# State-space input tables computed in their final position instead of being transposed

## The chip, the cores and the metric

The kernel runs on one core of a Trainium2 chip. The metric is device time in microseconds (us) of one execution: the median of three runs of the kernel before is 2120.89 us (2119.84 to 2126.75).

## What is computed

The reference is one layer of a hybrid decoder trunk on 256 tokens of width 2048: a SwiGLU feed-forward block, a mixer (a state-space model "S5" beside sparse attention), and a second feed-forward block, each between RMS norms. The change touches only the small tables of the S5 part. They depend on parameters alone, not on the tokens:

```python
dt = exp(log_dt); lam_re = min(a_re, -1e-4); mag = exp(lam_re * dt)
ab_re, ab_im = mag * cos(a_im * dt), mag * sin(a_im * dt)          # one complex factor per state
co_re, co_im = ((ab - 1) / lam)                                     # complex division, written out
bb_re = co_re[..., None] * b_re - co_im[..., None] * b_im
bb_im = co_re[..., None] * b_im + co_im[..., None] * b_re
bu = einsum('btgc,gpc->tbgp', ug, bb)                               # input of the recurrence
x = scan(x * ab + bu);  y = Re(einsum(x, c)) + d_skip * ug
```

There are 64 groups of 16 channels with 64 complex states each. The kernel takes four tokens at a time, so that its input table holds bb times the factor ab to the powers 3, 2, 1 and 0.

## The kernel before

All matmuls run as three products of split numbers: a weight tile ("raw", 128x1024 floats, 512 KB) is loaded by SyncE's queue (SP), ScalarE (ACT) rounds it into "hi" (line 103), VectorE (DVE) computes the rest "lo" (line 105), and TensorE (PE) multiplies hi and lo (lines 278 to 280). Below, **item n** is the n-th such weight tile of the stream; one item is 12 matmuls in the first stage. Five raw buffers and four pairs of hi and lo hold what is ahead, so the hi of item n can only be written when PE has finished item n-4.

The stages are: the first feed-forward block (a gate block and an up block of 8 items each for every 512 columns, then a down projection), the mixer, the second feed-forward block. In the first feed-forward block, while PE streams weights, a list of small steps called `background` is worked off by `pump`: one or two steps per item. The steps are the S5 parameters (`s5_params`, lines 742 to 819: some 90 VectorE instructions on 128x32, and two Sin on ScalarE), the attention bias table (`bias_table`: a load of 2 KB on ScalarE's queue, 12 small GpSimd instructions, a write and a 3 MB broadcast, lines 922 to 931), and then, for each of 8 column tiles `ct`:

- `loads` (lines 846 to 855): two loads of 128 KB, power 0 of the input table `bd`, the start of the output table `gb`;
- `b_power` three times (lines 860 to 862): the next power of `bd`, three VectorE instructions on 128x256 each;
- `into` (lines 871 to 876): 8 transposes of `bd` on PE (line 322), two copies from PSUM by ScalarE (line 875), a 512 KB write to `s5in` in DRAM;
- `c_power` four times (lines 867 to 869) and `out_of` (lines 884 to 896): 8 matmuls, two VectorE copies, 16 GpSimd copies into `hz` (line 892), three writes to `s5out`.

The mixer reads both tables back later. The gate block's Silu is line 690 and the product with the up block line 691; both read the PSUM banks `acc`, of which there are four, so that the third block (gate of the second 512 columns, items 17 to 24) can only start in a bank after line 690 has read it.

What sets the order of instructions on each engine is a scheduler at build time, which works with a model of the durations; each engine then runs its list strictly in that order. A DMA that ScalarE's queue issues stands in ScalarE's list too and holds up what follows while it waits.

```python
hl = self._pair()                                # 4 pairs of hi and lo
self.rounded.append(nc.scalar.activation(h, r, AF.Copy).ins)
self.rest = nc.vector.tensor_tensor(l, r, h.bitcast(F32), op=ALU.subtract).ins
pump(1 + (kk % 8 == 0))                          # steps of background per item
S.activation(sg, g[t], AF.Silu, scale=rr(t))     # frees the gate block's bank
```

Of the kernel before, what the change touches and what calls it, by code (L numbers as in the profile page):

```python
# [173 lines left out]
def body(tc, a):  # L174
# [651 lines left out]
    in_dram = dp.tile([8, 128, 1024], F32, name="s5in")  # L826
    out_dram = dp.tile([8, 128, 1536], F32, name="s5out")

    def s5_tables(sp_):
# [11 lines left out]
        state = {}  # L841

        def loads(ct):
# [4 lines left out]
            state["bd"] = sp_.tile([128, 2, 4, 4, 32], F32, name="bd")  # L848
            state["gb"] = sp_.tile([128, 2, 4, 5, 32], F32, name="gb")
            b0, bd, gb = state["b"], state["bd"], state["gb"]  # L850
            V.tensor_tensor(t1, b0, bc(cor, ct, False), op=ALU.mult)
            V.tensor_tensor(t2, b0[:, ::-1], bc(coi2, ct, True), op=ALU.mult)
            V.tensor_tensor(bd[:, :, :, 3, :], t1, t2, op=ALU.add)
# [16 lines left out]

        def into(ct):
            bt = sp_.tile([128, 2, 512], F32, name="bt")
            for r in range(2):
                p = transpose4(state["bd"][:, r].rearrange("p q j c -> p (q j c)"))
                S.activation(bt[:, r], p, AF.Copy)
            nc.scalar.dma_start(in_dram[ct], bt.rearrange("p r s -> p (r s)"))

        def out_of(ct):
# [3 lines left out]
            for q in range(4):  # L882
                for r in range(2):
                    T.matmul(hp[32 * q:32 * q + 32], bd[:, r, q, 3, :],
                             gb[:, r, q, 0:4, :], start=r == 0, stop=r == 1, tile_position=(0, 32 * q))
# [14 lines left out]
        def at_start(f):  # L900
            with tc.issue_after(start):
                f()

        background.append(lambda: at_start(s5_params))
        background.append(bias_table)
        for ct in range(8):
            background.append(lambda ct=ct: loads(ct) if ct else at_start(lambda: loads(0)))
            for j in (2, 1, 0):
                background.append(lambda ct=ct, j=j: b_power(ct, j))
            background.append(lambda ct=ct: into(ct))  # L910
# [521 lines left out]
def layout(i):  # L1432
# [7 lines left out]
    for n in ("ffn1", "ffn2"):  # L1440
# [23 lines left out]
    d["ssm_b"] = np.ascontiguousarray(np.stack(  # L1464
        [_block_diag(f["ssm_b_re"]), _block_diag(f["ssm_b_im"])], axis=2)).reshape(8, 128, 256)
    d["ssm_c"] = np.ascontiguousarray(np.stack(
        [_block_diag(f["ssm_c_re"].transpose(0, 2, 1)), _block_diag(f["ssm_c_im"].transpose(0, 2, 1))],
# [21 lines left out]
```

## Time and profile before

| | |
|---|---|
| runs | 2120.89, 2119.84, 2126.75 us |
| profiled execution, its own time | 2120.92 us |
| its span, first to last instruction | 2119.2 us |
| PE busy | 2096.6 us, 99% of the span |
| VectorE busy | 1572.3 us, 74% |
| ScalarE busy | 1115.5 us, 53% |
| granted TensorE clock, mean | 0.999 |
| moved by DMA | 437.63 MB, 207 GB/s |

Busy shares are averages over stages. Matmuls are pipelined, so the duration of one (0.39 us for 128x512) is longer than the distance from one start to the next, which is the price of one more matmul in a row. All other times below are in us from the span's start.

### The profile page before, as it was taken

Reading aid. Unit: us, or ns where it says so; the run is one execution under the profiler, and the core shown is the slowest. Engines: PE = TensorE matmul, PEld = TensorE weight load, DVE = VectorE, ACT = ScalarE, POOL = GpSimd, SP = SyncE. Lnnn points to the kernel's source line nnn. Section 1 sums busy time; section 2 is a strip of 40 time slices with the busy share of each in tenths; the row PEclk is TensorE's granted clock in tenths of the full one; section 3 lists DMA queues with packets and bytes.
Section 4 is the critical chain, followed back from the end, with each engine's and each line's share of the span. In section 5 each row is a group of like instructions: output and inputs, shape, how many; then the busy total and the mean of one; then the engine's idle time right before and its main releaser. Section 6 shows DMA issues by size and latency. Waiting matters only on the chain.

```text
span 2119.2 us, 27930 instructions
## 1 busy us (share of the span) xinstructions
PE 2096.6 (99%) x10048; PEld 1726.9 (81%) x10048; DVE 1572.3 (74%) x2268; ACT 1115.5 (53%) x1537; POOL 273.3 (13%) x494
## 2 busy tenths in 40 slices
PE   8999999999999999999999999999999999999998
PEld 7887788888888878998787778888878888888886
DVE  7898788886867864454456656577898889778676
ACT  6444455555555565554445554465555555555453
POOL 1222300000000002993104320000000000000000
PEclk9999999999999999999999999999999999999999
DMA  8877656565665766567754346676556665656665
GB/s 285 268 239 234 202 196 211 197 213 180 205 206 198 272 205 225 163 223 248 276 165 139 122 144 214 203 268 184 188 191 197 208 197 190 219 170 210 217 207 179
DMA packets 137146, 437.63 MB, mean 207 GB/s; under 512 B 14880, under 2 KB 27312, under 8 KB 136880
## 3 DMA queue, kind: packets, MB, share of 16 engines
q1 hardware_dynamic: 117504, 403.10, 58.0%
q10 hardware_dynamic: 19504, 32.75, 4.5%
q8 instruction: 79, 1.29, 0.2%
q14 instruction: 59, 0.48, 0.1%
HBM read 417.42 MB, written 21.52 MB: 207 GB/s over the span
## 4 chain that ended last, share of the span: by engine, by line
PE 81%; POOL 8%; DVE 5%; issue 2%; DMA 2%; ACT 1%; ACTq 0%; DVEq 0%; SPq 0%; POOLq 0%
PE bank L524 15%; PE bank L525 15%; PE bank L523 15%; PE acc L278 10%; PE acc L279 10%; PE acc L280 10%; DVE lo L105 2%; POOL st L1005 2%; POOL sc L1002 2%; PE xp L322 2%; POOL sc L1003 1%; POOL st L1004 1%; DMA raw<-in_ffn_gu 1%; POOL hz L892 1%; DMA s5out<-gb 1%
## 5 line engine op out<-in xcount | busy, mean ns | idle before, releaser
L105 DVE TENSOR_TENSOR lo<-raw,hi 128x1024 fp32r<-128x1024 f32 (+3 forms) x676 | 796.7, 1186 | 353.7 <-ACT hi L103 352.2
L103 ACT ACTIVATE hi<-raw 128x1024 fp32r<-128x1024 f32 (+3 forms) x676 | 686.1, 1023 | 682.1 <-PE acc L280 306.8
L278 PE MATMUL acc<-hi,ah 128*128 128x512 f32 (+2 forms) x1072 | 414.9, 388 | 2.0 <-ACT hi L103 1.9
L279 PE MATMUL acc<-lo,ah 128*128 128x512 f32 (+2 forms) x1072 | 413.9, 386 | 0.0
L280 PE MATMUL acc<-hi,al 128*128 128x512 f32 (+2 forms) x1072 | 412.6, 385 | 0.0
L524 PE MATMUL bank<-lo,ah 128*128 128x512 f32 x758 | 296.7, 391 | 2.3 <-DVE lo L105 2.3
L525 PE MATMUL bank<-hi,al 128*128 128x512 f32 x746 | 290.7, 390 | 0.0
L523 PE MATMUL bank<-hi,ah 128*128 128x512 f32 x758 | 282.0, 391 | 0.0
L278 PEld LDWEIGHTS acc<-hi,ah 128*128 128x128 f32 x1072 | 201.4, 188 | 42.8 <-ACT hi L103 2.7
L279 PEld LDWEIGHTS acc<-lo,ah 128*128 128x128 f32 x1072 | 201.7, 188 | 38.9 <-issue 2.1
L280 PEld LDWEIGHTS acc<-hi,al 128*128 128x128 f32 x1072 | 201.6, 188 | 38.3 <-DVE al L351 0.3
L524 PE MATMUL bank<-lo,hT 128*128 128x512 f32 x520 | 202.5, 389 | 0.0
L525 PE MATMUL bank<-hi,hT 128*128 128x512 f32 x520 | 202.3, 389 | 0.0
L523 PE MATMUL bank<-hi,hT 128*128 128x512 f32 x520 | 190.7, 390 | 0.1
L524 PEld LDWEIGHTS bank<-lo,ah 128*128 128x128 f32 x758 | 142.4, 188 | 32.5 <-DVE lo L105 3.5
L523 PEld LDWEIGHTS bank<-hi,ah 128*128 128x128 f32 x758 | 142.3, 188 | 29.3
L525 PEld LDWEIGHTS bank<-hi,al 128*128 128x128 f32 x746 | 140.1, 188 | 28.7
L103 ACT ACTIVATE hi<-sums 128x1024 fp32r<-128x1024 f32 x84 | 88.5, 1054 | 63.0 <-DVE sums L140 29.7
L523 PEld LDWEIGHTS bank<-hi,hT 128*128 128x128 f32 x520 | 97.5, 188 | 21.1 <-ACT hi L103 0.9
L524 PEld LDWEIGHTS bank<-lo,hT 128*128 128x128 f32 x520 | 97.6, 188 | 20.2
L525 PEld LDWEIGHTS bank<-hi,hT 128*128 128x128 f32 x520 | 97.6, 188 | 20.1
L105 DVE TENSOR_TENSOR lo<-sums,hi 128x1024 fp32r<-128x1024 f32 x84 | 101.0, 1217 | 3.9 <-ACT hi L103 3.1
(322 smaller groups left out, 2674.3 us busy)
## 6 DMA issues: line engine op xcount, KB each, us to landing
raw<-in_ffn_gu SPq DMA_DIRECT2D x352, 512.0 KB, 4.3
raw<-in_ffn_d SPq DMA_DIRECT2D x176, 512.0 KB, 4.3
raw<-in_w_ya SPq DMA_DIRECT2D x64, 512.0 KB, 3.4
raw<-in_w_in SPq DMA_DIRECT2D x40, 512.0 KB, 4.1
raw<-in_w_gate_b SPq DMA_DIRECT2D x32, 512.0 KB, 3.7
raw<-in_w_out SPq DMA_DIRECT2D x32, 512.0 KB, 3.8
raw<-in_w_o SPq DMA_DIRECT2D x16, 512.0 KB, 3.9
tab<-s5out ACTq DMA_DIRECT2D x8, 768.0 KB, 6.5
```

The source lines that it names most:

```text
L103: self.rounded.append(nc.scalar.activation(h, r, AF.Copy).ins)
L105: self.rest = nc.vector.tensor_tensor(l, r, h.bitcast(F32), op=ALU.subtract).ins
L278: T.matmul(o, lh, wh[:, k, :], start=kk + k == 0, stop=False)
L279: T.matmul(o, lh, wl[:, k, :], start=False, stop=False)
L280: last_product[0] = T.matmul(o, ll, wh[:, k, :], start=False, stop=kk + k == nk - 1).ins
L322: last_transpose[0] = T.transpose(p[:, k, :], src[:, k * cols:(k + 1) * cols], ident).ins
L523: T.matmul(out, lh, wh[:, j, :], start=key not in self.started, stop=False)
L524: T.matmul(out, lh, wl[:, j, :], start=False, stop=False)
L525: last_product[0] = T.matmul(out, ll, wh[:, j, :], start=False, stop=last).ins
L892: G.tensor_copy(hq[32 * j:32 * j + 32, q, j:, :], hs[32 * q:32 * q + 32, 0:4 - j, :])
L1002: G.tensor_tensor(w[:, 0], x, a4r2, op=ALU.mult)
L1005: G.tensor_tensor(y, y, w[:, 1], op=ALU.add)
```

## The change

The input table is computed in the position that the matmul wants, channels on partitions and states on the free axis. The inputs are laid out turned on the host (`ssm_bt`, repeated four times over the partitions, one copy for each power), and the complex factors, co times ab to the powers 0 to 3, are put into rows: `coefs` computes them for all groups at once (20 VectorE instructions on 128x32), transposes them with two matmuls, copies them three times by ScalarE (one of them negated) and writes 128x384 floats to `k_dram` ("s5k"). For each column tile, four loads on ScalarE's queue then broadcast a 6 KB row of it to 32 partitions each (`kt`), and one load of 512 KB brings the turned input (`bt0`). `into` becomes two halves of three VectorE instructions on 128x512. The 24 `b_power` steps, the 64 transposes and their 16 copies are gone. `coefs` stands before `bias_table` in the list.

```diff
+        def coefs():
+            w = work().rearrange("p (r j c) -> p r j c", r=4, j=4)
+            k, t = w[:, 0:2], w[:, 2:4]
+            tt = V.tensor_tensor
+            V.tensor_copy(k[:, 0, 3], cor)
+            V.tensor_copy(k[:, 1, 3], coi2[:, 1])
+            for j in (2, 1, 0):
+                xr, xi = k[:, 0, j + 1], k[:, 1, j + 1]
+                tt(t[:, 0, 0], xr, ar, op=ALU.mult)
...
+            p = transpose4(k.rearrange("p r j c -> p (r j c)"), n=2)
+            rows = work().rearrange("p (v s) -> p v s", v=4)
+            S.activation(rows[:, 0], p[:, 0], AF.Copy)
+            S.activation(rows[:, 1], p[:, 1], AF.Copy, scale=-1.0)
+            S.activation(rows[:, 2], p[:, 1], AF.Copy)
+            nc.scalar.dma_start(k_dram, rows[:, 0:3].rearrange("p v s -> p (v s)"))
...
+            nc.scalar.dma_start(state["bt"].rearrange("p r q s -> p (r q s)"), a["ssm_bt"][ct])
+            for j in range(4):
+                src = k_dram[32 * j + 4 * ct:32 * j + 4 * ct + 4].rearrange("q n -> (q n)")
+                nc.scalar.dma_start(state["k"][32 * j:32 * j + 32].rearrange("p q v s -> p (q v s)"),
+                                    src.unsqueeze(0).to_broadcast([32, 1536]))
...
-        def b_power(ct, j):
-            bd = state["bd"]
-            src = bd[:, :, :, j + 1, :]
-            V.tensor_tensor(t1, src, bc(ar, ct, False), op=ALU.mult)
-            V.tensor_tensor(t2, src[:, ::-1], bc(ai2, ct, True), op=ALU.mult)
-            V.tensor_tensor(bd[:, :, :, j, :], t1, t2, op=ALU.add)
...
-        def into(ct):
-            bt = sp_.tile([128, 2, 512], F32, name="bt")
-            for r in range(2):
-                p = transpose4(state["bd"][:, r].rearrange("p q j c -> p (q j c)"))
-                S.activation(bt[:, r], p, AF.Copy)
-            nc.scalar.dma_start(in_dram[ct], bt.rearrange("p r s -> p (r s)"))
+        def into(ct, half):
...
+            V.tensor_tensor(y, x[:, :, qs], k[:, qs, 0].unsqueeze(1).to_broadcast([128, 2, 2, 128]), op=ALU.mult)
+            V.tensor_tensor(t, x[:, ::-1, qs], k[:, qs, 1:3].rearrange("p q v s -> p v q s"), op=ALU.mult)
+            V.tensor_tensor(y, y, t, op=ALU.add)
+            if half:
+                nc.scalar.dma_start(in_dram[ct], state["in"].rearrange("p r q s -> p (r q s)"))
...
         background.append(lambda: at_start(s5_params))
+        background.append(coefs)
         background.append(bias_table)
```

The scheduler's lists move with it. Below are three places, first of ScalarE. This is ScalarE's list before from the load of the bias table on (`rel_bias`, line 922); the two lines 690 are the Silu of the gate block for the two token tiles:

```order
L922 DMA wk<-in_rel_bias 16x32
L350 ACTIVATE ah_135<-xp,gains 128x128
L103 ACTIVATE hi<-raw 128x1024
L690 ACT_TABLE_LOAD
L690 ACTIVATE wk<-acc,r_415 128x512
L930 DMA rb_one<-wk 16x384
L103 ACTIVATE hi<-raw 128x1024
L931 DMA rb<-rb_one 128x6144
L784 ACTIVATE wk<-wk 128x32
L103 ACTIVATE hi<-raw 128x1024
```

And this is ScalarE's list of the change up to the hi of item 21. The rows ahead of it are the hi of items 18 to 20, a load for the second column tile and the three copies of `coefs` (lines 862 to 864). Line numbers are the changed kernel's: 865 is the write of `coefs`, 879 a load of `kt`, 876 the load of `bt0` for the second column tile, 906 the write of `s5in`; 952 to 961 are the bias table:

```order
L952 DMA wk<-in_rel_bias 16x32
L865 DMA s5k<-wk 128x384
L690 ACT_TABLE_LOAD
L690 ACTIVATE wk<-acc,r_416 128x512
L690 ACTIVATE wk<-acc,r_429 128x512
L879 DMA kt<-s5k 32x1536 x4
L960 DMA rb_one<-wk 16x384
L961 DMA rb<-rb_one 128x6144
L876 DMA bt_850<-in_ssm_bt 128x1024
L879 DMA kt<-s5k 32x1536
L906 DMA s5in<-bt 128x1024
L103 ACTIVATE hi<-raw 128x1024
```

The first Silu stood right behind the hi of item 15; it now stands behind the hi of item 20, behind the copies and the write of `coefs`, with a second table load (one more stands at the Sin, line 784). Between the hi of item 20 and that of item 21 lie twelve DMA issues. Three more loads of `kt` follow behind the hi of item 21.

On PE this is the list of the change at the end of item 16 (the last of the first up block); in the list before, the same place reads the same without the row of line 322:

```order
L279 MATMUL acc<-lo,ah_136 128x512
L280 MATMUL acc<-hi,al_137 128x512
L322 MATMUL xp<-ident,wk 128x128 x2
L278 MATMUL acc<-hi,ah_134 128x512
L279 MATMUL acc<-lo,ah_134 128x512
```

The two transposes of `coefs` stand between item 16 and item 17, the first item of the next gate block.

On VectorE this is the list of the change from the lo of item 20 on (854 to 859 are `coefs`, 812 to 819 the end of `s5_params`):

```order
L105 TENSOR_TENSOR lo<-raw,hi 128x1024
L815 TENSOR_TENSOR a4r_112<-wk 128x32
L816 TENSOR_SCALAR a4i_113<-wk 128x32
L854 TENSOR_TENSOR wk<-wk,ar 128x32
L855 TENSOR_TENSOR wk<-wk,ai_109 128x32
L857 TENSOR_TENSOR wk<-wk,ai_109 128x32
L858 TENSOR_TENSOR wk<-wk,ar 128x32
L818 COPY a4r_112<-a4r_112 128x32
L819 TENSOR_SCALAR a4i_113<-a4i_113 128x32
L856 TENSOR_TENSOR wk<-wk 128x32
L859 TENSOR_TENSOR wk<-wk 128x32
L854 TENSOR_TENSOR wk<-wk,ar 128x32
```

Five more small instructions end `coefs`, so that it is done only 16 small instructions behind the lo of item 20. Behind it stand the two of line 691, the six of `into` of the first column tile (902 to 904), five of `c_power` on 128x256, and then the lo of item 21. Ahead of it, 17 instructions (15 on 128x32, two on 128x256) lie between the lo of item 19 and that of item 20, where before there were four.

## Rows read from the trace of the kernel before

**Rows 1.** The page's first part: busy time, share of the span and instructions of each engine.

```profile
PE 2096.6 (99%) x10048; PEld 1726.9 (81%) x10048; DVE 1572.3 (74%) x2268; ACT 1115.5 (53%) x1537; POOL 273.3 (13%) x494
```

**Rows 2.** The waits of PE alone over the whole span: line, what it waited for, us in total, times, longest.

```profile
PE xp L322 <- DMA wk<-in_x: 5.4, 2, 5.1
PE bank L524 <- DVE lo L105: 2.9, 4, 1.1
PE xp L322 <- DVE bd L862: 2.2, 1, 2.2
PE acc L278 <- ACT hi L103: 1.9, 2, 1.4
```

**Rows 3.** Busy time by stretch: length, then each engine's busy us (and instructions), granted clock, DMA share, GB/s. The stretch from 57 to 240 is that of the column tiles; 13 to 16 is the kernel's opening.

```profile
57.00:240.00 183.00, 180.75 (x940) 146.71 (x939) 158.62 (x312) 79.19 (x91) 47.59 (x113) 1.00 0.74 240
13.00:16.00 3.00, 3.00 (x19) 2.53 (x18) 2.23 (x6) 2.35 (x6) 0.00 (x0) 1.00 1.04 408
```

**Rows 4.** PE in order of time around the first group of eight transposes: start, duration, instruction.

```profile
70.62 0.39 PE L280 MATMUL acc<-hi,al 128*128 128x512 f32 x1
70.85 1.03 PE L322 MATMUL xp<-ident,bd 128*128 128x128 f32 x8
71.64 0.48 PE L278 MATMUL acc<-hi,ah 128*128 128x512 f32 x1
71.96 0.39 PE L279 MATMUL acc<-lo,ah 128*128 128x512 f32 x1
```

**Rows 5.** Groups of instructions from 0 to 420: times, busy us and mean ns of one, idle time before them.

```profile
L322 PE MATMUL xp<-ident,bd 128*128 128x128 f32 x64 | 8.3, 273 | 2.3 <-DVE bd L862 2.2
L860 DVE TENSOR_TENSOR t<-bd,ar 128x256 f32<-128x256 f32 x24 | 10.6, 440 | 0.1
L567 DVE TENSOR_TENSOR wk<-bank,wk 128x512 f32<-128x512 f32 x4 | 2.8, 692 | 0.7 <-PE bank L525 0.3
L350 ACT ACTIVATE ah<-xp,gains 128x128 fp32r<-128x128 f32 x32 | 11.1, 382 | 8.6 <-DVE al L351 4.4 <-PE xp L322 3.9
```

**Rows 6.** The time around the one idle stretch of PE in the column tiles, all engines: start, duration, instruction, and in brackets the idle time before it with its releaser.

```profile
212.56 11.51 POOL L892 COPY hz<-hs 32x32 f32<-32x32 f32 x16 [17.53 <-DVE hs L887]
224.56 2.95 ACT L103 ACTIVATE hi<-raw 128x1024 fp32r<-128x1024 f32 x3 [8.32 <-POOL hz L892]
225.65 1.23 DVE L105 TENSOR_TENSOR lo<-raw,hi 128x1024 fp32r<-128x1024 f32 x1 [4.82 <-ACT hi L103]
228.15 1.06 PE L322 MATMUL xp<-ident,bd 128*128 128x128 f32 x8 [2.22 <-DVE bd L862]
```

**Rows 7.** PE in order of time where item 16 ends and item 17 begins.

```profile
56.34 0.39 PE L280 MATMUL acc<-hi,al 128*128 128x512 f32 x1
56.57 0.39 PE L278 MATMUL acc<-hi,ah 128*128 128x512 f32 x1
```

**Rows 8.** ScalarE in order of time (ACTq is its queue issuing a DMA): the hi of item 15 and the first Silu with its table load, the hi of item 20, and a pair of DMA issues later on.

```profile
39.37 1.06 ACT L103 ACTIVATE hi<-raw 128x1024 fp32r<-128x1024 f32 x1 [0.28 <-PE acc L280]
40.44 1.28 ACT L690 ACT_TABLE_LOAD   x1
41.74 0.69 ACT L690 ACTIVATE wk<-acc,r 128x512 f32<-128x512 f32 x1
56.82 1.06 ACT L103 ACTIVATE hi<-raw 128x1024 fp32r<-128x1024 f32 x1 [1.08 <-PE acc L280]
119.28 0.94 ACTq L895 DMA_DIRECT2D s5out<-gb  x2
```

**Rows 9.** VectorE in order of time: an instruction on 128x256 and what follows, small ones in a row, and the lo of item 19 with what follows it.

```profile
53.94 0.42 DVE L851 TENSOR_TENSOR t<-ld,cor 128x256 f32<-128x256 f32 x1
54.28 0.18 DVE L804 TENSOR_TENSOR wk<-wk 128x32 f32<-128x32 f32 x1
54.50 0.19 DVE L805 TENSOR_TENSOR coi<-wk 128x32 f32<-128x32 f32 x1
54.61 0.19 DVE L814 TENSOR_TENSOR wk<-ar,ai 128x32 f32<-128x32 f32 x1
55.44 1.22 DVE L105 TENSOR_TENSOR lo<-raw,hi 128x1024 fp32r<-128x1024 f32 x1
56.58 0.74 DVE L691 SCALAR_TENSOR_TENSOR wk<-acc,r,wk 128x512 f32<-128x512 f32 x1
```

**Rows 10.** PE in order of time in its first stretch of matmuls, after it had been idle.

```profile
10.01 0.63 PE L280 MATMUL acc<-hi,al 128*128 128x512 f32 x1
10.43 0.63 PE L278 MATMUL acc<-hi,ah 128*128 128x512 f32 x1
10.86 0.61 PE L279 MATMUL acc<-lo,ah 128*128 128x512 f32 x1
```

**Rows 11.** DMA issues over the whole span: times, KB each, median us from issue to landing; and the landing times of the writes of `s5out`, least, median and greatest.

```profile
s5out<-gb ACTq DMA_DIRECT2D x16, 256.0 KB, 4.4
rb_one<-wk ACTq DMA_DIRECT2D x1, 24.0 KB, 2.1
wk<-in_rel_bias ACTq DMA_DIRECT2D x1, 2.0 KB, 3.3
DMA to landing us min/median/max: 2.0/4.2/7.1
```

**Rows 12.** GpSimd on the bias table, in order of time.

```profile
40.44 3.63 POOL L928 TENSOR_SCALAR wk<-wk 16x5 f32<-16x5 f32 x11
```

More of the change, by code (lines that the diff above doesn't have):

```diff
@@ L827, in body @@
     out_dram = dp.tile([8, 128, 1536], F32, name="s5out")
+    k_dram = dp.tile([128, 384], F32, name="s5k")
     def s5_tables(sp_):
@@ L847, in loads @@
                 state[nm] = w
[L848 removed]
+            state["bd"] = sp_.tile([128, 2, 4, 32], F32, name="bd")
             state["gb"] = sp_.tile([128, 2, 4, 5, 32], F32, name="gb")
[L850 removed]
+            state["bt"] = sp_.tile([128, 2, 4, 128], F32, name="bt0")
+            state["k"] = sp_.tile([128, 4, 3, 128], F32, name="kt")
+            nc.scalar.dma_start(state["bt"].rearrange("p r q s -> p (r q s)"), a["ssm_bt"][ct])
[3 more added lines that the diff above has]
+                                    src.unsqueeze(0).to_broadcast([32, 1536]))
+            b0, gb = state["b"], state["gb"]
             V.tensor_tensor(t1, b0, bc(cor, ct, False), op=ALU.mult)
             V.tensor_tensor(t2, b0[:, ::-1], bc(coi2, ct, True), op=ALU.mult)
[L853 removed]
+            V.tensor_tensor(state["bd"], t1, t2, op=ALU.add)
             V.tensor_copy(gb[:, 0, :, 0, :], state["c"][:, 0])
             V.tensor_scalar(gb[:, 1, :, 0, :], state["c"][:, 1], -1.0, None, op0=ALU.mult)
[L857 to L862 removed]
         def c_power(ct, k):
@@ L869, in c_power @@
             V.tensor_tensor(gb[:, :, :, k, :], t1, t2, op=ALU.subtract)
-        def into(ct):
-            bt = sp_.tile([128, 2, 512], F32, name="bt")
-            for r in range(2):
-                p = transpose4(state["bd"][:, r].rearrange("p q j c -> p (q j c)"))
-                S.activation(bt[:, r], p, AF.Copy)
-            nc.scalar.dma_start(in_dram[ct], bt.rearrange("p r s -> p (r s)"))
+        def into(ct, half):
+            if half == 0:
+                state["in"] = sp_.tile([128, 2, 4, 128], F32, name="bt")
+            qs = slice(2 * half, 2 * half + 2)
+            x, k, y = state["bt"], state["k"], state["in"][:, :, qs]
+            t = t12.rearrange("p a r q c -> p (a r q c)").rearrange("p (r q s) -> p r q s", r=2, q=2)
+            V.tensor_tensor(y, x[:, :, qs], k[:, qs, 0].unsqueeze(1).to_broadcast([128, 2, 2, 128]), op=ALU.mult)
[3 more added lines that the diff above has]
+                nc.scalar.dma_start(in_dram[ct], state["in"].rearrange("p r q s -> p (r q s)"))
         def out_of(ct):
@@ L883, in out_of @@
                 for r in range(2):
-                    T.matmul(hp[32 * q:32 * q + 32], bd[:, r, q, 3, :],
+                    T.matmul(hp[32 * q:32 * q + 32], bd[:, r, q, :],
                              gb[:, r, q, 0:4, :], start=r == 0, stop=r == 1, tile_position=(0, 32 * q))
@@ L907, in s5_tables @@
             background.append(lambda ct=ct: loads(ct) if ct else at_start(lambda: loads(0)))
-            for j in (2, 1, 0):
-                background.append(lambda ct=ct, j=j: b_power(ct, j))
-            background.append(lambda ct=ct: into(ct))
+            for half in range(2):
+                background.append(lambda ct=ct, half=half: into(ct, half))
             for k in range(1, 5):
@@ L1465, in layout @@
         [_block_diag(f["ssm_b_re"]), _block_diag(f["ssm_b_im"])], axis=2)).reshape(8, 128, 256)
+    d["ssm_bt"] = np.ascontiguousarray(np.stack([np.tile(_block_diag(f["ssm_b_" + r]).transpose(0, 3, 2, 1), (1, 4, 1, 1))
+                                                 for r in ("re", "im")], axis=2)).reshape(8, 128, 1024)
     d["ssm_c"] = np.ascontiguousarray(np.stack(
```

5 lines of the change are left out of this document (added).

## The prediction

> **What bounds the kernel now.** The first part of the page comes first: TensorE is busy for 99% of the span [rows 1]. That alone could hide stages with another limit, so its waits are next: over the whole span they name a wait of 5.4 us at the opening, and the three largest others sum to 7.0 us, none of them longer than 2.2 us at a time [rows 2]. PE is the bound in the stage of the tables too: from 57 to 240 it is busy for 180.75 of 183 us, at full granted clock, while VectorE has 158.62 and ScalarE 79.19 [rows 3]. Two things follow. An instruction taken from PE's row shortens the run by what it holds up in that row. And a new wait of PE lengthens it one to one, since no later stage has slack to give back.
>
> **1. The 64 transposes.** The price is not their duration. A group of eight shows 273 ns for one [rows 5], but the starts tell what the row loses: a matmul ahead starts at 70.62, the group at 70.85, so a step is 0.23; the second matmul behind the group starts at 71.96 and would without it have started at 70.85 + 0.23 = 71.08 [rows 4]. A group costs 0.88 us, eight cost **7.0 us**, all in PE's row: -7.0. Their 16 copies go from ScalarE and the 24 steps of `b_power` from VectorE; neither was what PE waited for [rows 2], with one exception.
>
> **2. The exception.** At 228.15 PE had been idle for 2.22 us and stood at transposes whose input VectorE delivered late, because ScalarE had waited 8.32 us in its list for GpSimd's `hz` [rows 6]. The transposes are gone, the wait for `hz` is not: the hi that it held up started at 224.56, and its lo ended at 225.65 + 1.23 = 226.88, where PE, idle since 228.15 - 2.22 = 225.93, would still have had to wait. So 228.15 - 226.88, about **1.2 us**, goes: -1.2. Bounds: 0 (another wait there) and 2.2.
>
> **3. VectorE in the tables.** Out go 72 instructions on 128x256 at about 440 ns, 32 us; in come 48 on 128x512 at about 692 ns, 33 us [rows 5]. It has 24 us of slack in that stretch [rows 3]. Price 0; if the cover fails it is the 1.5 us of difference.
>
> **4. PE waits at the new transposes: +9.6.** This is the place that decides. The lists show that the two transposes of `coefs` stand behind item 16 on PE, and that `coefs` ends on VectorE only behind the lo of item 20. But the hi of item 20 needs the buffer of item 16: before, it starts at 56.82, released by PE [rows 8], just as item 16's last matmul, started at 56.34, is through [rows 7]. So when PE arrives at the transposes, the hi, the lo and the rest of `coefs` that stand ahead of their input are still to be done, one after the other. In steps, from rows:
> - Lo of item 19 at 55.44, the next instruction at 56.58 [rows 9]. Then 15 small ones at 0.11 (54.61 less 54.50) and two on 128x256 at 0.34 (54.28 less 53.94) [rows 9]: 2.3, so 58.9. The lo of item 20 takes 1.1: 60.0. Sixteen small ones, a few of which wait for the one ahead (0.22, as 54.50 less 54.28 [rows 9]): 2.1, so 62.1.
> - Two transposes and the way to ScalarE, 0.5; three copies on 128x128 at 0.38 [rows 5], 1.1; the issue of the write, 0.4; so 64.1.
> - PE's next instruction, item 17, needs the bank that the Silu empties. In the new list that Silu stands behind all this: table load 1.28 and Silu 0.69, back to back [rows 8]: 66.1.
> PE goes on at 66.2 where it went on at 56.57 [rows 7]: **+9.6**. Bounds: 8.0, if the copies and small instructions overlap better; 10.5, if every dependent one takes 0.22.
>
> On the table load a rule speaks against the change. Before, the hi ahead of it ends at 39.37 + 1.06 = 40.43, and the Silu starts at 41.74 [rows 8], so a load costs 1.3 us here. The Trainium skill (ScalarE: Activation LUTs, section "What ACT_TABLE_LOAD costs") gives 1.28 us for the load and about 1.38 us for a drain, 2.66 in all for every switch of sets. By the page, the sum below would be 1.4 us higher. This case's trace shows no drain, and the sum keeps 1.3.
>
> **5. PE's slow start: +1.6.** After the idle time at the opening the starts of matmuls lie 0.43 apart (10.01, 10.43, 10.86) [rows 10] against 0.23 later [rows 4]. The wait ahead of that was 5.1 us [rows 2], and the new one is longer. Taken, whatever its reason: about 8 matmuls at 0.2 more, +1.6; bounds 0 and 1.6.
>
> **6. ScalarE is held up once more: +2.2.** Behind the Silus its list has twelve DMA issues, some of which wait, ahead of the hi of item 21. The write of `coefs`, issued at 64.1, lands some 4 us later (between 2.1 for 24 KB and 4.4 for 256 KB [rows 11]): 68.1. Four loads of `kt` at 0.47 an issue (0.94 for two [rows 8]): 70.0; the last lands 4.4 later: 74.4. Meanwhile the bias table: its load lands 3.3 after 63.8 [rows 11], GpSimd takes 3.9 [rows 12], the write 2.1: 73.1, just covered. Then VectorE does `into` for the first column tile, which waits for `kt`, 6 x 0.69 [rows 5]: 78.5. ScalarE's load of `bt0` and write of `s5in` wait for that; the hi of item 21 ends at 80.0. Its lo stands behind five instructions on 128x256 (1.7) and takes 1.2: 81.4. PE has items 17 to 20 to work on, 48 matmuls at 0.23, and the slow start: 66.2 + 10.9 + 1.6 = 78.7, and two matmuls that need the hi alone. So PE waits again for about **2.2**. Bounds: 0, if the loads land in 2.1; 5, if they take the 7.1 of the slowest write [rows 11].
>
> **7. Each column tile.** ScalarE's queue issues 11 DMAs instead of 6, 5 x 0.47 = 2.3 us more, in one block around the wait for `hz`. What covers it: four pairs ahead are 4 x 2.7 us of PE, less one hi and one lo, 8.6 us. Before, only the wait of 8.32 came near that. Price 0, with rival A for the rest. The bytes: 10.7 MB more over 183 us are 58 GB/s on top of 240, and the opening moved 408 [rows 3].
>
> **The sum**, against the profiled execution's own 2120.92 us (its span plus 1.7; the median of the runs is 2120.89, the same): -7.0 - 1.2 + 9.6 + 1.6 + 2.2 = +5.2, so **2126.1 us**. Three runs of this kernel differ by up to 0.3%, 6.4 us, which is about what a measurement can tell from no change; the forecast is slightly slower, but inside that. With its bounds the case runs from 2119 (8.0 - 7.0 - 2.2) to 2131 (10.5 + 1.6 + 5 - 7.0).
>
> **Rivals.**
> - *A, slower: the block of DMA issues in every column tile.* For seven tiles the hi behind the wait for `hz` comes 2.3 us later. It decides once that wait and the issues pass 8.6 us. For it: the wait was 8.32 once, and PE idled [rows 6]. Against it: PE idled only that once. At full effect 7 x 2.3 = 16.5 on the sum: 2142; at half, 2134.
> - *B, faster: PE is not held at item 16*, because VectorE and ScalarE run further ahead than in the trace. For it: the scheduler chose the order. Against it: the buffer of item 16 is a true dependence, and the hi was released by PE [rows 8]. With terms 4 to 6 at 0: 2112.7; at a quarter, 2116.
> - *C, slower: the second table load costs twice its 1.28*, since ScalarE empties its pipeline around it. It would put the Silu and PE 1.3 us later: 2127.4. Against it stands the back-to-back start [rows 8]. (It is the rule of the Trainium skill in part 4, ScalarE: Activation LUTs.)
>
> **How the numbers follow.** The forecast's case has 0.67 (same 0.43, slower 0.23, faster 0.01), since its sum lies near the upper border; A 0.20 (slower 0.16, same 0.04); B 0.10 (faster 0.09, same 0.01); C 0.03 (slower). Together: faster 0.10, same 0.48, slower 0.42. The range reaches from 2114, into B, to 2139, most of A.
>
> **What would show it.** In the profile of the changed kernel: PE idle for 9 to 10 us from about 57 at line 322 and then at line 278, put down to VectorE's `coefs` and to the Silu; matmul starts 0.43 apart for some 3 us behind it; a second wait of 0 to 5 us near 79 for the lo of item 21; no transposes of `bd`; and from 85 to 240 PE idle for no more than 3 us. If PE is idle for less than 4 us between 55 and 85, part 4 is wrong. If it idles repeatedly beyond 85 for ScalarE's hi, A is right.

## The result, and the profile after

The change takes 2152.44 us (median of five runs, 2151.35 to 2154.89) against 2120.72 of the kernel before: a ratio of 1.0149, with a 95% interval of 1.0131 to 1.0166, or 31.7 us more. Forecast were 2126.1, with 2139 as the upper end of the range. The profiled execution took 2151.35 us, with a span of 2149.5, which is 30.3 more than the span before.

Busy time hardly differs from [rows 1]; the sum of PE's waits does. First part of the page, and the waits of PE alone over the whole span (line, what it waited for, us in total, times, longest; line numbers from here on are those of the kernel named, and the changed kernel's L690 and L103 are still the Silu and hi):

```profile
PE 2102.8 (98%) x9986; PEld 1724.9 (80%) x9986; DVE 1577.3 (73%) x2264; ACT 1106.9 (51%) x1525; POOL 294.2 (14%) x494
```

```profile
PE acc L278 <- ACT hi L103: 15.0, 10, 3.6
PE acc L279 <- DVE lo L105: 6.9, 7, 2.4
...
PE xp L322 <- DVE wk L856: 4.6, 1, 4.6
PE acc L278 <- ACT wk L690: 3.1, 1, 3.1
```

In [rows 2] the hi cost 1.9 us and bd 2.2. Now 15.0 and 6.9 us go to hi and lo that come late, one piece at a time, and 4.6 + 3.1 to the new transposes and the Silu behind them. By stretch (columns as in [rows 3]: length, busy us and instructions of PE, PEld, DVE, ACT, POOL, then granted clock, DMA share, GB/s):

```profile
57.00:70.00 13.00, 5.33 (x14) 3.90 (x14) 6.13 (x34) 4.22 (x7) 2.88 (x12) 0.63 0.64 177
70.00:85.00 15.00, 15.00 (x66) 12.18 (x64) 14.05 (x24) 5.20 (x5) 0.00 (x0) 0.98 0.85 255
85.00:180.00 95.00, 83.53 (x396) 64.84 (x395) 70.50 (x126) 28.52 (x32) 38.33 (x64) 0.93 0.89 281
180.00:245.00 65.00, 58.89 (x292) 45.66 (x293) 54.76 (x96) 24.38 (x27) 24.54 (x36) 1.00 0.86 269
245.00:310.00 65.00, 62.62 (x292) 50.91 (x291) 51.62 (x67) 31.71 (x38) 14.07 (x29) 1.00 0.65 209
```

Length less PE busy is PE's idle time: 7.7 us from 57 to 85, 11.5 from 85 to 180, 8.5 from 180 to 310, where the kernel before has 0, 0 and 3.4. What the clock costs can't be read off the rows in the same way, because part of the time at the lower level falls into these idle stretches. Counting matmuls tells both at once. The n-th matmul of line 280 on `acc` (1344 in either trace) starts later in the change than before by 0.4 us at 57 (the change's time), 10.6 at 85, 18.2 at 105, 27.4 at 145, 30.7 at 245 and 30.2 at 310. So all of the 30.3 arises here. The start has 10.2 of it, or 11.1 with the 0.9 for the one group of transposes that the kernel before runs in this time. The tiles have 19.6, or 25.8 if the other seven groups are worth 0.88 us each. So the start was near what was forecast, and the tiles, priced at nothing, cost some 20 us net, and some 26 with what the transposes give back.

**The start.** PE in order of time, beside [rows 7]:

```profile
56.70 0.39 PE L280 MATMUL acc<-hi,al 128*128 128x512 f32 x1
61.65 0.69 PE L322 MATMUL xp<-ident,wk 128*128 128x128 f32 x2 [4.56 <-DVE wk L856]
65.44 0.79 PE L278 MATMUL acc<-hi,ah 128*128 128x512 f32 x1 [3.11 <-ACT wk L690]
66.04 0.63 PE L279 MATMUL acc<-lo,ah 128*128 128x512 f32 x1
66.46 0.63 PE L280 MATMUL acc<-hi,al 128*128 128x512 f32 x1
...
70.72 0.39 PE L278 MATMUL acc<-hi,ah 128*128 128x512 f32 x1
70.95 0.39 PE L279 MATMUL acc<-lo,ah 128*128 128x512 f32 x1
```

PE stands at the transposes until VectorE's coefs are done and then at line 278 until the Silu, and goes on at 65.44 (forecast: 66.2). The starts lie 0.42 to 0.43 apart until 70.72 and 0.23 behind that. The first is the lower of the clock's two levels, 1.2 GHz (the granted clock is 0.50 from 66 to 70), the second 2.4.

**The first tile stall.** ScalarE and then VectorE in order of time (ACTq issues a DMA; brackets: idle time before, releaser):

```profile
63.41 1.28 ACT L690 ACT_TABLE_LOAD   x1 [0.42 <-ACT wk L864]
64.70 0.69 ACT L690 ACTIVATE wk<-acc,r 128x512 f32<-128x512 f32 x1
...
81.83 1.06 ACT L103 ACTIVATE hi<-raw 128x1024 fp32r<-128x1024 f32 x1 [1.66 <-PE acc L280]
90.70 1.47 ACTq L925 DMA_DIRECT2D s5out<-gb  x2
95.28 0.36 ACTq L870 DMA_DIRECT2D ld<-in_ssm_b  x1
95.69 1.09 ACT L651 ACTIVATE hT<-xp 128x512 fp32r<-128x512 f32 x2 [12.80 <-DMA s5out<-gb]
```

```profile
85.15 0.42 DVE L883 TENSOR_TENSOR t<-ld,coi 128x256 f32<-128x256 f32 x1
95.33 1.29 DVE L902 TENSOR_TENSOR bt<-bt,kt 128x512 f32<-128x512 f32 x2 [9.77 <-DMA raw<-in_ffn_gu]
96.54 0.24 DVE L917 SCALAR_TENSOR_TENSOR hs<-fold,dsk,xp 128x32 f32<-128x32 f32 x1
```

Both engines stop for some 10 us. ScalarE has no hi to give between 82.9 and 96.7, since three DMA issues that wait stand ahead. VectorE stands at the first product of the next tile, which needs kt; the releaser named is a weight load, though the product reads bt and kt, and the last load of kt, issued at 76.31, landed at 95.21. Over the tiles, the largest waits of ScalarE for transfers and for hz, and then of SP's queue for table loads (57 to 280; those left out above and between them are for other engines):

```profile
ACT hi L103 <- DMA kt<-s5k: 26.1, 3, 9.7
...
ACT hi L103 <- POOL hz L922: 16.1, 2, 13.0
ACT hT L651 <- DMA s5out<-gb: 12.8, 1, 12.8
ACT wk L690 <- DMA s5in<-bt: 11.7, 1, 11.7
...
ACT hi L103 <- DMA s5in<-bt: 8.9, 1, 8.9
```

```profile
SPq L94 <- DMA bt<-in_ssm_bt: 18.2, 5, 4.5
SPq L94 <- DMA kt<-s5k: 16.5, 4, 5.9
```

In the kernel before, ScalarE had 1.0 us of waits for a table transfer in this stretch and SP none. The second fence tells why a table can hold up a weight: the program gives SP's and ScalarE's transfers eight semaphores in turn, and an issue waits until the earlier transfer on its own has landed. At the first stall the landings in the trace show it one by one: the weight load issued at 83.56 stood until the 3 MB of the bias table (issued at 70.88) had landed at 83.51, those at 87.21 and 88.30 until bt0 (87.16) and a kt (88.24); ScalarE's two writes of gb, at 90.70 and 91.80, until s5in (90.63) and a kt (91.78), and its load at 95.28 until the last kt (95.21). ScalarE's list of one tile, with its waits, shows them:

```
L876 DMA bt_1042<-in_ssm_bt 128x1024 [waits DVE_49]
L879 DMA kt<-s5k 32x1536 [waits DMAHW5_49,DMAHW2_49]
L926 DMA s5out<-hz_442 128x512 [waits DMAHW3_49,Pool_49]
L870 DMA ld<-in_ssm_c 128x256 [waits DMAHW5_49,DVE_49]
L906 DMA s5in<-bt 128x1024 [waits DMAHW6_49,DVE_49]
L879 DMA kt<-s5k 32x1536 [waits DMAHW7_49]
L879 DMA kt<-s5k 32x1536 [waits DMAHW0_49]
L879 DMA kt<-s5k 32x1536 [waits DMAHW1_49]
```

The chain of waits from 140 to 215, by engine and line, first before, then after (the view cuts the lines at their ends):

```profile
by line: POOL hz L892 20.0%; DVE lo L105 17.4%; issue 15.5%; DMA s5out<-gb 8.2%; DVE t L868 6.2%; DVE gb L869 6.1%; DMA raw<-in_ffn_gu 5.7%; DVE t L867 3.2%; ACTq L895 2.9%; ACT hi L103 2.8%; DVE wk L486 2.6%; DVE t L861 2.6%; DVE bd L862 2
```

```profile
by line: DMA s5out<-gb 29.9%; DMA kt<-s5k 16.4%; issue 8.6%; DVE lo L105 6.7%; DMA ld<-in_ssm_b 6.5%; DVE gb L893 5.3%; DMA raw<-in_ffn_gu 4.2%; ACTq L925 4.1%; ACTq L879 3.7%; DMA ld<-in_ssm_c 3.5%; DVE t L891 2.8%; DVE t L892 2.5%; POOL h
```

Before, the chain runs through GpSimd's copies and VectorE's work. After, more than half of it is transfers on their way: 29.9 + 16.4 + 6.5 + 4.2 + 3.5 = 60.5%. They also land later (issues from 57 to 260: KB each, median us to landing; a write of gb took 4.4 in [rows 11], a weight load 4.2 in the same stretch before):

```profile
raw<-in_ffn_gu SPq DMA_DIRECT2D x56, 512.0 KB, 5.2
kt<-s5k ACTq DMA_DIRECT2D x32, 192.0 KB, 6.6
bt<-in_ssm_bt ACTq DMA_DIRECT2D x7, 512.0 KB, 6.0
s5out<-gb ACTq DMA_DIRECT2D x14, 256.0 KB, 6.4
```

### The profile page after: what moved, and what is told of

Same layout as the page of the kernel before. It is cut to its first block, busy times and chain, and to the rows that moved or that the text cites. A ratio compares the mean times of both kernels' runs of the same rounds, so it can differ in the third digit from the quotient of the medians.

```text
span 2149.5 us, 27845 instructions
## 1 busy us (share of the span) xinstructions
PE 2102.8 (98%) x9986; PEld 1724.9 (80%) x9986; DVE 1577.3 (73%) x2264; ACT 1106.9 (51%) x1525; POOL 294.2 (14%) x494
## 3 DMA queue, kind: packets, MB, share of 16 engines
q8 instruction: 78, 1.28, 0.3%
## 4 chain that ended last, share of the span: by engine, by line
PE 75%; DMA 7%; POOL 7%; DVE 6%; issue 3%; ACT 1%; ACTq 0%; DVEq 0%; POOLq 0%; SPq 0%
PE bank L524 14%; PE bank L525 14%; PE bank L523 14%; PE acc L278 9%; PE acc L279 9%; PE acc L280 9%; DVE lo L105 2%; DMA kt<-s5k 2%; DMA raw<-in_ffn_gu 2%; POOL st L1035 2%; POOL sc L1032 2%; PE xp L322 1%; POOL sc L1033 1%; POOL st L1034 1%; DMA s5out<-gb 1%
## 5 line engine op out<-in xcount | busy, mean ns | idle before, releaser
L103 ACT ACTIVATE hi<-raw 128x1024 fp32r<-128x1024 f32 (+3 forms) x676 | 684.2, 1023 | 694.9 <-PE bank L525 285.1
L279 PEld LDWEIGHTS acc<-lo,ah 128*128 128x128 f32 x1072 | 203.4, 190 | 49.8 <-DVE lo L105 11.1
L103 ACT ACTIVATE hi<-sums 128x1024 fp32r<-128x1024 f32 x84 | 88.4, 1054 | 61.3 <-DVE sums L140 29.2
```

The lines of the kernel that those rows point to most:

```text
L279: T.matmul(o, lh, wl[:, k, :], start=False, stop=False)
```

## The experiments

Each time is given as its difference to the kernel before, run beside it (2117.3 to 2119.4 us), with the 95% interval of the ratio. The change itself stands at +31.7. "The tables end" means the last copy into hz: at 249 before, at 275 in the change.

### The hold at the start

**Coefs added to the kernel before (e14).**
```diff
+        background.append(coefs)
         background.append(bias_table)
```


> The kernel before with coefs added (its 20 VectorE instructions, two transposes, three copies, the write of the rows) ahead of the bias table, and nobody reads the rows. Parts 4 and 5 of the forecast by themselves: PE is held 7 to 8 us near 60 and runs some 5 us slower after it, 2129 to 2133 against 2118, with the tiles undisturbed behind it. If the hold is taken in by later slack: 2118 to 2123.

Measured: +11.0 us (1.0039 to 1.0066), inside the first range, and as much as the 11.1 us of the change's own trace. PE's waits from 57 to 310:

```profile
PE xp L322 <- DVE wk L854: 6.0, 1, 6.0
PE xp L322 <- DVE bd L884: 2.6, 2, 2.1
PE acc L278 <- ACT wk L690: 0.6, 1, 0.6
```
That is 6.6 us of idle time at the start, with a granted clock of 0.61 from 57 to 70. The hold is shown, by itself.

**Coefs later (e1).**
```diff
+        background.append(bias_table)
+        background.extend([lambda: None] * 8)
         background.append(coefs)
-        background.append(bias_table)
```


> The change with the factor rows (coefs) emitted eight steps later in the background list and behind the bias table, so that PE's two transposes of them and ScalarE's copies stand behind the first Silu, which is again right behind the hi of item 15. Everything else is as in the change. Theory H (PE is held at these transposes and at the late Silu, 4.6 + 3.1 us, and then runs 13 us at a granted clock of 0.63, some 4.8 us more): about 12.5 us below the change's 2152.4, so 2140, with the idle stretches behind 85 us still there. Theory T (the stalls of the column tiles are the whole story): 2150 to 2153.

Measured: +33.6 us (1.0142 to 1.0170). The hold is gone, and the time is not. The tables end at 287, and what the start gave back is lost at the end. The row from 245 to 310, and ScalarE's wait at line 496 there (the sums for the first fast block, whose pool takes the tables' memory):

```profile
245.00:310.00 65.00, 54.50 (x245) 41.68 (x244) 50.19 (x77) 26.49 (x32) 15.50 (x38) 0.92 0.62 194
```
```profile
ACT sh L496 <- DMA s5out<-hz: 13.8, 1, 13.8
```
PE is idle for 10.5 of these 65 us, at a mean granted clock of 0.92. The time is in theory T's range, but e14 shows that the stalls of the tiles are not the whole story. Neither theory had the loss at the end; it is theory C below: the end of the tables' chain sets the time.

**Transposes by VectorE (e10).** On top of e7 below, bias table first:
```diff
-            p = transpose4(...); S.activation(rows...) x2; nc.scalar.dma_start(k_dram, ...)
+            V.transpose(rows[:, 0:2]..., k...)       # blocks of 32x32
+            nc.scalar.dma_start(kd[b, :, v], rows[32 * b:32 * b + 32, v])      # 8 writes
```


> The version with two rows and two buffers of kt, with the bias table first, and the factor rows transposed by VectorE (one 128x256 instruction in blocks of 32x32) and written by eight small DMAs, so that neither PE nor ScalarE's copies take part: PE is not held near 60, and the chain of the tiles does not start later for it. Theory H (the hold of 7.5 us and 5.1 us of clock, on top of the rest): 2132.7 less 10 to 13, 2120 to 2123. Theory C (the end of the tables' chain, after which the first block with sums of weights can begin, sets the time, whatever PE does before): 2127 to 2134.

Measured: +19.9 us (1.0081 to 1.0118), more than e7 and above both ranges. The trace is of the longest of its four executions (2143.9 against 2138.2 to 2138.4). In it PE, which no longer takes part in coefs, still stopped from 57 to 85:

```profile
60.62 0.50 PE L278 MATMUL acc<-hi,ah 128*128 128x512 f32 x1 [3.20 <-ACT wk L690]
...
78.64 0.79 PE L279 MATMUL acc<-lo,ah 128*128 128x512 f32 x1 [3.37 <-DVE lo L105]
```
```profile
ACT wk L690 <- DMA s5k<-wk: 8.3, 1, 8.3
```
The Silu now stands in ScalarE's list behind the eight writes, which wait for VectorE. The hold lies in the lists, not in PE's two transposes.

### The column tiles

**Another queue (e2).** `nc.scalar` becomes `nc.gpsimd` at the two load lines of the tiles.


> The change with the five loads of each column tile (turned input and four factor rows) issued by GpSimd's queue in place of ScalarE's. Same bytes, same start. Theory Q (ScalarE's list stops at these issues, so that its hi come late, idle PE 20 us in all behind 85 us and lower the clock, some 7 us more): the stretch from 85 to 260 has no more idle time of PE than the 3.3 us of the kernel before, and the time falls by 16 to 24 us to 2129 to 2136. Theory B (the 10.7 MB more on the DMA engines make the landings late, whoever issues them): within 5 us of 2152. The idle 7.7 us near 60 stay in both.

Measured: +35.3 us (1.0152 to 1.0180). Theory Q falls in its plain form: PE still waits 12.3 us for hi and lo behind 85, and the tables end at 283. GpSimd's list issues a tile's loads behind the 16 copies of the tile ahead. The time is in theory B's range. From 57 to 300 ScalarE has no wait for a load of kt or bt0 left and SP only 0.6 us for a table transfer, so those waits, large as they are in the change, don't make its loss by themselves.

**One load of kt (e3).**
```diff
-            for j in range(4):
-                src = k_dram[32 * j + 4 * ct:...]; dma_start(state["k"][32 * j:32 * j + 32], ...)
+            dma_start(state["k"], k_dram[4 * ct:4 * ct + 4]... broadcast to [128, 1536])
```


> The change with one load of the factor rows per column tile in place of four: the row of power 0 is broadcast to all 128 partitions (the other powers are left out, so the tables are not those of the reference). Same bytes, 24 issues on ScalarE's queue fewer in the tiles. If the number of issues and of transfers that each must wait for is what holds ScalarE: 10 to 20 us less, 2133 to 2142. If the bytes do, or the waits of the two writes in the same block (for GpSimd's hz, for VectorE's product): 2147 to 2153.

Measured: +21.8 us (1.0091 to 1.0118), 9.9 less than the change at the same bytes, and inside the first range. The count of transfers matters.

**Few bytes (e5).** `kt` is 32x192 a load, `bt0` 128x128.


> The change with the same loads on ScalarE's queue, but each brings an eighth of its row (kt 32x192, bt0 128x128), and VectorE's products read one value of it, repeated, so that the tables are not those of the reference; 9.4 of the 10.7 MB are left out, no issue is. Theory B (the bytes on the DMA engines) and theory L (each tile waits for the landing of loads that are issued late, and landing grows with size): the idle time of PE behind 85 us and the clock that goes with it (some 24 us) mostly go, 2129 to 2138. Theory Q' (the number of issues and of semaphores to wait for): 2147 to 2153. The hold at the start stays in all.

Measured: +18.7 us (1.0069 to 1.0114), 13.0 less at the same count: the bytes matter too. The time is in the range of theories B and L, which this run does not tell apart. Weight loads land earlier again (median 4.7 us from 57 to 260), the writes of gb do not (6.8), so it is not the bytes alone that make those late.

**Both (e17).**


> The change with one load of factor rows per tile in place of four and an eighth of the bytes in it and in the turned input (e3 and e5 together; the values are not those of the reference). If count and bytes are two causes that add up: 2152 - 13 - 15 = 2124, which is the kernel before, less 7 of transposes, plus 12 of the hold, so that the tiles cost nothing more. If they are one cause that either removes: 2135 to 2138.

Measured: +12.8 us (1.0043 to 1.0076), 18.9 less, where a plain sum gives 22.9. The time lies between the two expectations; count and bytes mostly add up. What is left is the hold and some waits in the lists (PE, 57 to 310):

```profile
PE acc L279 <- DVE lo L105: 7.4, 11, 1.1
PE xp L322 <- DVE wk L856: 4.3, 1, 4.3
PE acc L278 <- ACT wk L690: 3.1, 1, 3.1
```

**The same bytes on the kernel before (e6).** Six loads a tile on GpSimd's queue that nobody reads.


> The kernel before, with the transposes and all, plus the same bytes per column tile in six loads on GpSimd's queue (four broadcasts of a 6 KB row to 32 partitions, two of 256 KB) that nobody reads. Theory B (more traffic makes all landings late): 2130 to 2142. Theory L (it is that the tile's chain waits for them): 2117 to 2122, with at most 3 us for GpSimd's own issues.

Measured: +14.9 us (1.0039 to 1.0086), in theory B's range. But the trace doesn't show that the bytes cost anything beside the tiles. Matched by count as above, PE is 7.7 us behind the kernel before at 40 already and 8.3 behind at 275. It lost this in the opening: GpSimd issues the first tile's loads from 1.9 us on, and the loads of the input x land after 11.4 us (median) in place of 6.7. In the change no load of kt falls there. GpSimd, whose copies into hz stand behind these loads, also waits 67 us for its own two buffers. The profiled execution was the shortest of the four (2127.1 against 2131.5 to 2135.2), and the rest of the 14.9 is not in its trace. So this run neither shows theory B for the tiles nor refutes theory L.

**Two rows, two buffers (e7).**
```diff
-            state["k"] = sp_.tile([128, 4, 3, 128], F32, name="kt")
+            state["k"] = sp_.tile([128, 4, 2, 128], F32, name="kt", tag="kt", bufs=2)
...
-            V.tensor_tensor(y, y, t, op=ALU.add)
+            V.tensor_tensor(y[:, 0], y[:, 0], t[:, 0], op=ALU.subtract)
+            V.tensor_tensor(y[:, 1], y[:, 1], t[:, 1], op=ALU.add)
```


> The change with two rows of factors (real and imaginary, the sign by a subtract in place of the add) instead of three, 4.2 instead of 6.3 MB, and two buffers of kt, so that its loads need not wait for the product of the tile before. Theory L, with the wait for the buffer as the reason that the loads are issued late: 10 to 20 us less, 2132 to 2142. If the loads are late only by their place in ScalarE's list, behind the write of hz: 2146 to 2152, the bytes alone.

Measured: +14.3 us (1.0047 to 1.0084), 17.4 less than the change and inside the first range: the best form of it. What the buffer and what the 2.1 MB less did is not told apart; at e5's rate, 13.0 us for 9.4 MB, the bytes would be worth some 3 us, an estimate.

**One load on top of that (e18).**


> The version with two rows and two buffers of kt (e7, 2132.7) with one load of kt per tile in place of four (the row of power 0 for all partitions, so the tables are not the reference's). If the count of transfers holds ScalarE's list even when the buffer is free: 2122 to 2128. If with two buffers the loads are early enough: 2130 to 2135.

Measured: +15.3 us (1.0060 to 1.0090), the same as e7 and in the second range. With a tile's loads issued ahead, their count no longer shows in the time.

**Bias table first (e9).** The two lines `coefs` and `bias_table` swapped.


> The change with two lines of the background list swapped: the bias table stands ahead of coefs, so that its 3 MB broadcast (rb, issued at 70.9 in the change, 12.6 us to land) is issued some 20 us earlier, as before the change, and no longer stands in the queue ahead of the loads of kt for the second tile, which took up to 18.9 us to land. Theory R (this collision makes the one stall of 12.8 us on ScalarE at 83 to 96, 4.9 us of idle PE and some 3 us of slow clock): 2152 less 7 to 10, so 2142 to 2145. If the later tiles only wait more instead: 2149 to 2153. The hold of PE near 60 stays.

Measured: +32.1 us (1.0132 to 1.0177), in the second range: theory R falls. The loads of kt for the second tile did land early. First the change (70 to 100), then e9 (70 to 110), least, median and greatest:

```profile
DMA to landing us min/median/max: 13.7/17.3/18.9
```
```profile
DMA to landing us min/median/max: 4.2/5.6/5.9
```
Yet PE idles 11.7 us from 85 to 180, as in the change. The stall near 97 is gone (matched by count, PE is 10.4 us behind the kernel before at 105, where the change has 18.2), but others took its place (28.9 at 245).

**Two buffers of gb (e13).** On e7, the product in place in `bt0`, work pool of 12.


> The version with two rows and two buffers of kt (2132.7), with two buffers of gb as well; the product is made in place in the turned input's tile to make room, and the work pool has 12 buffers in place of 13. Theory L in its last form (each tile waits for the landing of the tile before: of the writes of gb, 5.5 to 8.7 us, and of s5in): the next tile's first copy no longer waits for them, PE's idle time from 85 to 245 falls from 7.9 us to under 3, and the time to 2122 to 2128. If VectorE's list alone sets the pace of the tiles: 2130 to 2135.

Measured: +19.2 us (1.0073 to 1.0101), more than e7 and above both ranges. VectorE's copy into gb still waits:

```profile
DVE gb L884 <- DMA s5out<-gb: 13.9, 5, 5.1
```
So a single buffer was not that wait's reason, or not the only one; the copy also reads a load that ScalarE issues behind others. Three things were changed at once here, and why it is slower stays open.

### The transposes, and the end of the tables

**Left out (e4).**
```diff
-                p = transpose4(state["bd"][:, r]...)
-                S.activation(bt[:, r], p, AF.Copy)
+                S.activation(bt[:, r], state["bd"][:, r]..., AF.Copy)
```


> The kernel before with the 64 transposes of the input table left out: ScalarE copies bd itself to bt (so the input table is not turned). Nothing else changes. This is term 1 by itself (7.0 us) with the exception of term 2 (1.2): 2112.5 against 2120.7, between 2110 and 2115. If the transposes cost by their durations, 8.3 us: much the same. If they lie beside other work and cost PE nothing: 2120.

Measured: +0.1 us (0.9992 to 1.0014), as in the last of the three cases, but for another reason. The tables end at 248, no earlier than before, and PE, now ahead, waits for them (PE from 245 to 310, then ScalarE):

```profile
PE bank L523 <- ACT sh L496: 3.2, 1, 3.2
```
```profile
ACT sh L496 <- DMA s5out<-hz: 8.5, 1, 8.5
```
Of the 9.4 us that PE is ahead of the kernel before at 245, 4 are gone at 300. This execution (2114.2) lies 3.3 under the median of the eleven (2113.8 to 2122.7), so its trace shows only a part of what took the gain back.

**Copies into hz on ScalarE (e12).** `G.tensor_copy` becomes `S.activation(..., AF.Copy)`.


> The kernel before with its 16 copies into hz of each tile on ScalarE in place of GpSimd, nothing else. Theory C: the chain of a tile is shorter by 3 to 6 us, its end comes earlier than PE needs it, and the one idle stretch of 2.2 us near 228 goes: 2113 to 2118 against some 2118. If ScalarE's copies hold up the hi: 2119 to 2126.

Measured: -0.4 us (0.9989 to 1.0008). The tables end at 238, PE has no wait from 57 to 310, and the time is the same: the chain was not late enough to cost more than 2 us.

**Both (e15).**


> The kernel before with the copies into hz on ScalarE (2118.1, its tables end 10 us before the first block with sums of weights begins) and the 64 transposes left out as in e4 (the input table is not turned). Theory C (in e4 the end of the tables' chain took the gain back): now the 7.0 us of term 1 show, 2109 to 2113. If the transposes cost PE nothing: 2116 to 2120.

Measured: -5.8 us (0.9967 to 0.9988, that is 2.5 to 7.0 us), 4.5 below e12's median, or 5.4 by the two differences, and just above the first range. The transposes are worth 4.5 to 5.8 us where the tables end early (at 240 here), and nothing that can be measured in e4, where they don't. This bears theory C out.

### Other versions

**Copies into hz on VectorE (e8).** In the change, `G.tensor_copy` becomes `V.tensor_copy`.


> The change with the 16 copies into hz of each tile on VectorE in place of GpSimd, where they took 5.7 to 11.5 us a tile before and take 7.7 to 14.9 us in the change (a copy takes 0.25 us, but as long as VectorE's instruction where one of those on 128x512 or 128x1024 runs beside it). Theory G (the chain of a tile, and with it ScalarE's list, waits for these copies, and the wider products made them slower): 12 to 22 us less, 2130 to 2140. If the landing of kt alone decides: 2147 to 2153; and VectorE has 16 x 8 small copies more, some 14 us beside PE.

Measured: +40.6 us (1.0162 to 1.0210), 8.9 worse than the change and above both ranges. Theory G falls in this form: the tables end at 294.

**e10 with loads on GpSimd's queue and hz on ScalarE (e11).**


> The same, with the loads of kt and of the turned input on GpSimd's queue and the copies into hz on ScalarE, so that GpSimd only issues loads and ScalarE's list holds no wait for GpSimd and no load of kt. Theory C with the chain shortened by GpSimd's 8 to 15 us a tile: the last tile ends some 10 us earlier, 2112 to 2120, below the kernel before. If ScalarE's 16 copies a tile (3 to 4 us) delay the hi instead: 2122 to 2132.

Measured: +24.5 us (1.0103 to 1.0135), above both ranges. GpSimd's issue of the next turned input now waits 138.8 us in seven tiles for VectorE's last product from the one before (its line 903), since bt0 has one buffer. The tables end at 276, as in the change.

**e13 with late coefs and hz on ScalarE (e16).**


> All of it together: coefs eight steps later and behind the bias table (no hold of PE), two buffers of kt and gb, product in place, copies into hz on ScalarE. No idle time of PE from 57 to 240 beyond 3 us. The tables start some 15 us later than in the kernel before, so the first block with sums of weights waits for their end: theory C gives 2118 to 2128; if that end is early enough, the 7 us of the transposes show, 2111 to 2116.

Measured: +22.2 us (1.0090 to 1.0118), above both ranges. No hold, but 12.4 us of idle PE from 245 to 310, as in e1. No version of the change came below the kernel before.

## Why the prediction was wrong

- *Part 1, transposes, -7.0:* about right in size (e15: 4.5 to 5.8), and it shows only if nothing else waits at the end of the tables (e4: nothing). So it was wrong that what is taken from PE's row shortens the run in any case.
- *Part 2, -1.2:* the wait for hz stayed, as supposed, and its longest grew from 8.3 to 13.0 us. Whether the 1.2 us went can't be told in the change, where PE waits for other things from 180 to 245; in e12, without that wait, the time is the same.
- *Part 3, VectorE, 0:* right as busy time. But its list now has a product that waits for a load, and lo and hs stand behind it.
- *Parts 4 and 5, hold and slow start, 9.6 + 1.6 = 11.2:* 11.1 in the trace, 11.0 alone (e14). The mechanism was right. That the sum came out so closely was partly luck: PE stood for 8.5 us in place of 9.6, and the slow start cost 2.5 in place of 1.6, which was also its upper bound. It was taken at 8 matmuls, as many as one could guess from [rows 10]; it lasted for twelve, from 65.4 to 70.7.
- *Part 6, +2.2:* 0. PE was busy for 15.00 of 15.00 us from 70 to 85. The hi of item 21 came at 75.4 instead of ending at 80.0, because the loads of kt landed earlier than supposed.
- *Part 7, each column tile, 0:* this is the step that failed, by some 20 us net, and some 26 with what the transposes give back. It counted the time of the issues (2.3 us a tile) and the bytes (58 GB/s on 240). It did not count that each issue may wait for a landing of 5 to 7 us, that these stand in the list ahead of the hi, and that VectorE waits for the same loads. Weight loads wait in turn, 34.7 us on SP, but e2, without these waits, took as long. The cover of 8.6 us, which part 7 itself gave as the point of decision, was passed by waits of 9.7, 11.7, 12.8 and 13.0 us.
- *Rival A* was the right direction and place, with 0.20 as its chance, and too small: at full effect 16.5, for the issues alone. Its own test ("if it idles repeatedly beyond 85") came out. *Rival B* fell with e14. *Rival C* fell: the table load at 63.41 took 1.28 us, and the Silu started at 64.70. The 2.66 us of the Trainium skill (ScalarE: Activation LUTs, "What ACT_TABLE_LOAD costs") do not show here; the measurement decides.

Shown are the hold, the worth of the transposes, and that count and bytes of the new loads make most of the tiles' loss: without them (e17) the kernel stands 1.8 us above the hold alone (e14), so that what is left of the loss is about what the transposes give back. Not shown is by which wait they do it, since e2 and e9 each took away one that looked large, and the time stayed. The split of e7 between buffer and bytes, and the last 6 to 8 us of waits in e17, are not settled.

## What to carry to other kernels

A DMA that stands in a compute engine's list costs what it may wait for, not its issue: count, for each new transfer, the landing it waits for, the buffer it fills and the shared semaphore it takes, and compare the whole block with the cover ahead of PE. A stall, or work of PE, that went from one place (e1, e9, e4) gave nothing here while the chain that ends last was no shorter, so follow that chain to its end before pricing a gain. And when a value is moved from an engine to a load, look whether the load can be issued one round ahead; with a second buffer and fewer bytes (e7) the change lost half of its price.

## What the runs showed of the hardware that was not expected

GpSimd's small copies are slowed by VectorE. All 128 copies into hz from 57 to 300: busy us, mean ns, idle time, before, in the change, and on ScalarE in e12, each of the first two with the least, median and greatest duration in ns:

```profile
L892 POOL COPY hz<-hs 32x128 f32<-32x128 f32 (+3 forms) x128 | 55.3, 432 | 149.2 <-DVE hs L887 142.3
L892 POOL COPY hz<-hs x128: 205/287/6808, 79.3 to 248.4; 32x32 f32<-32x32 f32 x32, 32x128 f32<-32x128 f32 x32, 32x96 f32<-32x96 f32 x32, 32x64 f32<-32x64 f32 x32
```
```profile
L922 POOL COPY hz<-hs 32x128 f32<-32x128 f32 (+3 forms) x128 | 76.9, 601 | 131.1 <-DVE hs L917 124.2
L922 POOL COPY hz<-hs x128: 206/296/10350, 96.9 to 274.7; 32x32 f32<-32x32 f32 x32, 32x128 f32<-32x128 f32 x32, 32x96 f32<-32x96 f32 x32, 32x64 f32<-32x64 f32 x32
```
```profile
L892 ACT ACTIVATE hz<-hs 32x64 f32<-32x64 f32 (+3 forms) x128 | 34.3, 268 | 8.1 <-DVE hs L887 6.6
```
A copy with no VectorE instruction beside it takes 249 ns on average before (49 of the 128) and 250 in the change (31). The others are longer, and a few are very long: the one of 10.35 us, from 238.9, lies beside a row of VectorE's instructions without a gap. Such copies make most of the step in the mean from 432 to 601 ns. The wider products alone don't: e17 has them too, and a mean of 419. The Trainium skill (SBUF — State Buffer, "SBUF: two separate sides") states that a GpSimd instruction that reads SBUF and a VectorE instruction with two SBUF inputs exclude each other for a whole instruction; the rows agree with it, and ScalarE's 268 ns, beside the same VectorE, too.

After each of two longer stops in the first 110 us, of 4.6 + 3.1 and of 3.4 + 1.5 us, PE's starts lay 0.43 apart in place of 0.23 (the lower clock level), from 65.4 to 70.7 and from 100.3 to 104.7. At 0.43 for 0.23, 5.3 and 4.4 us lose 2.5 and 2.0: a third to two fifths of the stop on top of it.
